# The last MLP's second matrix with activations stationary, and its residual with tokens on partitions

## The chip, the cores and the metric

The kernel runs on one core of one Trainium2 chip. The metric is the device time of one execution in microseconds (us). Three runs of the kernel before took 2691.77, 2692.02 and 2692.03 us; the median, 2692.02 us, is the time that the change is held against.

## The reference

A trunk of two layers over 256 tokens of width 2048, in float32. Each layer is a modulated RMS norm, a mixer (layer 0: gated DeltaNet heads beside band attention; layer 1: a Mamba-2 SSD mixer) with a gated residual, then another norm and a squared-ReLU MLP with a gated residual. The change touches only the second half of the last MLP:

```python
def sq_relu_mlp(h, w1, w2):                 # w1 2048 x 8192, w2 8192 x 2048
    a = jax.nn.relu(jnp.einsum('btd,df->btf', h, w1))
    return jnp.einsum('btf,fd->btd', a * a, w2)
...
        h = rms_norm(x, norm_mlp_w[layer]) * (1.0 + sc2) + sh2
        x = x + g2 * sq_relu_mlp(h, mlp_w1[layer], mlp_w2[layer])
```

The gate `g2` has one value for each of the 2048 features and is the same for all tokens.

## The kernel before

**Split operands.** Every large product runs in two parts for precision. A weight tile `raw` (128 x 2048 numbers, 1 MB, one DMA on the queue of SP) is split in two halves of 1024 columns: ACT casts `wh` (L342), DVE subtracts `wl = raw - wh` (L346). Activations are held in the same way as a high and a low part in a tile `u`. The product is high x high, high x low and low x high, so three products for each pair of tiles. All matmuls of such products are recorded at L332.

**One chunk of the last MLP.** A chunk is one `raw` tile: eight blocks of 128 rows by 256 columns. `c_item` (L592) works it off with the weights stationary: for each row block and each of two column blocks, one matmul `wh` against high and low activations side by side (512 columns move), and one `wl` against the high part (256 columns move). That is 16 matmuls of 512 columns and 16 of 256, and 32 weight loads. `c_blocks` pairs two chunks (rows r = 0 and r = 1) for one output block of 256 features, `pw`, which has features on partitions and tokens along the row. In chunk r = 0 the order is `wh`, then `wl`; in chunk r = 1 it is `wl`, then `wh`, so the trace shows runs of 32 matmuls of each kind.

**The MLP's loop** (`mlp`, L1516). The 8192 hidden features go by in four parts f. In each part, 16 chunks of `w1` make eight tiles `a` (each `relu2`: L1525 ACT, L1526 DVE, two ACT squares, a cast and a DVE subtraction), and 16 chunks of `w2` add to the output. The last MLP so has 64 chunks of `w1` and 64 of `w2`. The residual (`residual`, L951) is done for every output block in every f: four DVE instructions `x = pw * gate + x` at L958, where the gate is a column of numbers, one for each partition. In the last f the blocks go out by DMA (L960).

**Order of the work.** A chunk's load and split are emitted one chunk ahead of its matmuls. `raw` tiles, and the tiles `mraw` of the modulation (`mod_job`, a 1 MB load at L463 and one DVE product at L466 each), share one pool of four buffers; a load is issued when DVE has let go of the buffer four loads back. `wh` has four buffers, `wl` five. The modulation that ends in the gate of this MLP, `mod[2, ("mlp", 1)]`, is spread over f = 0: 16 loads, `pump` issues one about every four ticks, and `need` forces it when a residual wants columns that are not ready. Small jobs that PE, DVE and ACT do between chunks are Python generators, stepped from a list `bg` while the matmuls are emitted; a scheduler then sets the place of each instruction on its engine. SP issues DMAs strictly in its own order. The program gives SP's DMAs eight completion counters in turn, and a DMA first waits until the last one that had its counter has landed.

**The end.** The last chunk does all matmuls of its first column block, then the residual of that block, then the second column block. Both column blocks lie in one tile `pw`, two banks of PSUM.

Of the kernel before, what the change touches and what calls it, by code (L numbers as in the profile page):

```python
# [10 lines left out]
F32 = mybir.dt.float32  # L11
# [101 lines left out]
class Trunk:  # L113
# [88 lines left out]
    def back(self, gen):  # L202
        t = Task(gen)
        self.bg.append(t)
        return t
# [345 lines left out]
        self.emit(Item(load.finish, run, after, self.still > 0))  # L551
        self.still -= 1

    def a_item(self, ps, src, act, first, last, after=None, whole=False):

        load, ws = self.loader(src, whole)

        def run():
            o_, (u, x) = ps(), act()
            for hf, (wh, wl) in enumerate(self.tiles(ws, 512)):  # L560
                for n in range(4):
                    k, t = (n % 2, n // 2) if last and hf else (n // 2, n % 2)
# [385 lines left out]
        return get  # L948


    def residual(self, ps, cb, key, last, final=False, fs=(0, 1)):  # L951

        nc = self.nc
        self.need(2, key, 2 * cb + 2)
        g, x, b = self.mod[2, key], self.x[cb // 2], cb % 2
        for f in fs:
            for n in range(2):
                self.last = nc.vector.scalar_tensor_tensor(x[:, 2 * b + f], ps[:, f, n], g[:, 2 * cb + f : 2 * cb + f + 1], x[:, 2 * b + f], op0=ALU.mult, op1=ALU.add)  # L958
            if final:
                nc.sync.dma_start(self.out[cb // 2, :, b * 512 + f * 256 : b * 512 + f * 256 + 256], x[:, 2 * b + f])  # L960
        if last and not final:
# [554 lines left out]
    def mlp(self, layer, acts, after=None):  # L1516

        nc = self.nc
        w1, w2 = self.i["w1"][layer], self.i["w2"][layer]
        NF = DFF // 2048  # L1520

        def relu2(ps, early):
            p = self.unit(F32R, [P, 2, 2, SEQ])
            lo = self.s2([P, 2, SEQ], tag="rs")
            nc.scalar.copy(lo, ps[:, :, 1])  # L1525
            nc.vector.tensor_tensor(lo, ps[:, :, 0], lo, op=ALU.add)  # L1526
# [33 lines left out]
    def mlp_rate(self, layer):  # L1560
        self.rate = 0.377 if layer == 0 else 0.25
# [226 lines left out]
def pack(inputs):  # L1788
# [4 lines left out]
    def chunks(w, width=512):  # L1793
# [50 lines left out]
```

## Time and profile before

| what | value |
|---|---|
| median of three runs | 2692.02 us |
| the profiled execution | 2691.54 us |
| its span (first to last instruction of the program) | 2689.8 us |
| PE busy | 2635.2 us, 98% of the span |
| DVE busy | 2151.9 us, 80% |
| ACT busy | 1348.2 us, 50% |
| granted TensorE clock | 0.999 |

The profile is one execution. A span of busy time is not a rate: matmuls overlap, so each record of a 512-column matmul lasts about 390 ns while one starts every 227 ns. Where the text needs a rate, it takes the distance between starts. "Idle before" is the time in which an engine did nothing ahead of an instruction, with the instruction that let it go on. SPq is the queue of SP, which only issues DMAs; a DMA's landing is told in the list of DMAs.

### The profile page before, as it was taken

The numbers are of one execution on the slowest core, as the hardware profiler recorded it, in microseconds if no ns is written. First come the engines' busy times: TensorE is split into PE (matmuls) and PEld (weight loads), VectorE is DVE, ScalarE is ACT, GpSimd is POOL, SyncE is SP. The second block draws the span as 40 slices with busy tenths as digits, with TensorE's granted clock in tenths as the row PEclk, the third lists the DMA queues.
The fourth block names the chain that finished last, engine by engine and source line by source line (L and its number), as shares of the span: only waits on it lengthen the run. The fifth ranks groups of instructions, "written<-read, shape, count | busy, mean of one in ns | idle before, by whom it ended". The sixth has DMA issues, their size and how long they took to land.

```text
span 2689.8 us, 40012 instructions
## 1 busy us (share of the span) xinstructions
PE 2635.2 (98%) x15834; PEld 2324.1 (86%) x15834; DVE 2151.9 (80%) x3106; ACT 1348.2 (50%) x1990; POOL 24.3 (1%) x98
## 2 busy tenths in 40 slices
PE   5999999999999999999999999999999999999999
PEld 4887989988888888888888888888888888888888
DVE  7998998997888888889889876888797855555554
ACT  3445455456345354454556544655455354453452
POOL 1000000000000000000000000000000000000000
PEclk9999999999999999999999999999999999999999
DMA  9986487868899898988566655655567855555553
GB/s 344 352 327 234 170 307 275 322 235 293 313 345 328 328 332 330 333 331 312 179 207 220 219 204 185 207 175 188 208 236 293 325 188 188 188 188 188 191 193 134
DMA packets 100459, 680.08 MB, mean 253 GB/s; under 512 B 11184, under 2 KB 14512, under 8 KB 19376
## 3 DMA queue, kind: packets, MB, share of 16 engines
q1 hardware_dynamic: 95376, 669.07, 68.6%
q10 hardware_dynamic: 4896, 8.46, 1.0%
q8 instruction: 124, 2.03, 0.3%
q14 instruction: 63, 0.52, 0.1%
HBM read 675.33 MB, written 2.16 MB: 252 GB/s over the span
## 4 chain that ended last, share of the span: by engine, by line
PE 90%; DVE 7%; ACT 2%; issue 1%; DMA 1%; DVEq 0%; SPq 0%; ACTq 0%
PE pw L332 71%; PE pg L332 12%; PE pm L335 3%; PE pm L332 2%; DVE wl L346 2%; DVE mraw L466 2%; PE pm L339 1%; DVE u L1619 0%; ACT wh L342 0%; DVE hf L893 0%; DVE u L1017 0%; DMA raw<-in_w_ab_dram 0%; ACT pm L1075 0%; DVE u L896 0%; ACT pm L1218 0%
## 5 line engine op out<-in xcount | busy, mean ns | idle before, releaser
L346 DVE TENSOR_TENSOR wl<-raw,wh 128x1024 fp32r<-128x1024 f32 x870 | 1053.8, 1223 | 433.4 <-ACT wh L342 430.9
L342 ACT CAST wh<-raw 128x1024 fp32r<-128x1024 f32 x870 | 905.0, 1050 | 980.8 <-PE pw L332 676.6
L332 PE MATMUL pw<-u,wh 128*128 128x512 f32 x5584 | 1318.8, 391 | 2.6 <-DVE u L896 1.3
L332 PEld LDWEIGHTS pw<-u,wh 128*128 128x128 f32 x5584 | 1032.5, 188 | 209.3 <-issue 1.9
L332 PEld LDWEIGHTS pw<-u,wl 128*128 128x128 f32 x5584 | 702.1, 191 | 21.0 <-DVE wl L346 1.1
L332 PE MATMUL pw<-u,wl 128*128 128x256 f32 x5584 | 711.0, 283 | 0.7 <-DVE wl L346 0.7
L466 DVE SCALAR_TENSOR_TENSOR mraw<-mraw,crow 128x2048 f32<-128x2048 f32 x192 | 438.8, 2287 | 8.6 <-DMA mraw<-in_mod_dram 8.4
L332 PE MATMUL pg<-wh,u 128*128 128x512 f32 x864 | 282.1, 398 | 0.0
L332 PEld LDWEIGHTS pg<-wh,u 128*128 128x128 f32 x864 | 162.0, 188 | 33.2 <-issue 1.0
L958 DVE SCALAR_TENSOR_TENSOR x<-pw,mod,x 128x256 f32<-128x256 f32 x352 | 161.9, 480 | 32.4 <-PE pw L332 30.0
L332 PE MATMUL pg<-wl,u 128*128 128x512 f32 x432 | 169.7, 393 | 0.4 <-DVE wl L346 0.2
L332 PE MATMUL pg<-u,wh 128*128 128x256 f32 x672 | 124.5, 286 | 0.0
L332 PEld LDWEIGHTS pg<-u,wh 128*128 128x128 f32 x672 | 105.5, 192 | 0.3
L332 PEld LDWEIGHTS pg<-wl,u 128*128 128x128 f32 x432 | 81.3, 188 | 18.2 <-DVE wl L346 1.9
L332 PE MATMUL pg<-u,wl 128*128 128x256 f32 x336 | 95.6, 284 | 0.1
L332 PE MATMUL pm<-u,wh 128*128 128x256 f32 (+1 forms) x340 | 64.1, 292 | 19.2 <-ACT wh L342 19.2
L332 PEld LDWEIGHTS pm<-u,wh 128*128 128x128 f32 x340 | 54.3, 199 | 20.3 <-ACT wh L342 20.0
L332 PEld LDWEIGHTS pg<-u,wl 128*128 128x128 f32 x336 | 64.4, 192 | 0.3 <-DVE wl L346 0.3
L1017 DVE SCALAR_TENSOR_TENSOR u<-pad,cst,u 128x256 f32<-128x256 f32 x144 | 61.6, 481 | 1.0 <-ACT u L1011 0.7
L1525 ACT COPY rs<-pw 128x512 f32<-128x512 f32 x64 | 36.8, 576 | 34.5 <-PE pw L332 34.5
L895 ACT ACTIVATE u<-hf,mod 128x256 fp32r<-128x256 f32 x64 | 29.3, 501 | 47.2 <-DVE hf L893 47.2
L1526 DVE TENSOR_TENSOR rs<-pw,rs 128x512 f32<-128x512 f32 x64 | 43.9, 686 | 9.9 <-ACT rs L1525 9.9
(298 smaller groups left out, 1520.5 us busy)
## 6 DMA issues: line engine op xcount, KB each, us to landing
raw<-in_w_dram SPq DMA_DIRECT2D x256, 1024.0 KB, 5.4
mraw<-in_mod_dram SPq DMA_DIRECT2D x192, 1024.0 KB, 6.3
raw<-in_w_ab_dram SPq DMA_DIRECT2D x56, 1024.0 KB, 6.3
raw<-in_w_ssd_dram SPq DMA_DIRECT2D x48, 1024.0 KB, 4.8
raw<-in_w_sz_dram SPq DMA_DIRECT2D x32, 1024.0 KB, 4.9
raw<-in_wo_ssd_dram SPq DMA_DIRECT2D x32, 1024.0 KB, 4.9
raw<-in_wo_ab_dram SPq DMA_DIRECT2D x16, 1024.0 KB, 6.0
sE<-sd_rowd ACTq DMA_DIRECT2D x32, 256.0 KB, 3.9
```

Source lines behind the costliest of these rows:

```text
L332: return self.nc.tensor.matmul(o, a, b, start=start, stop=stop, skip_group_check=True)
L335: self.nc.tensor.matmul(o, lhsT, rhs, start=True, stop=True, skip_group_check=True)
L339: return self.nc.tensor.transpose(o, a, self.anti if flip else self.ident[:k, :k])
L342: a = self.nc.scalar.copy(hi, src)
L346: b = self.nc.vector.tensor_tensor(lo, src, hi.bitcast(F32), op=ALU.subtract)
L466: x = nc.vector.scalar_tensor_tensor(raw, raw, 1.0, self.crow, op0=ALU.mult, op1=ALU.mult, accum_out=t[:, f : f + 1])
L895: nc.scalar.activation(hi, h[:, f], AF.Identity, bias=shift[:, col])
L958: self.last = nc.vector.scalar_tensor_tensor(x[:, 2 * b + f], ps[:, f, n], g[:, 2 * cb + f : 2 * cb + f + 1], x[:, 2 * b + f], op0=ALU.mul ...
L1017: nc.vector.scalar_tensor_tensor(h, pad[:, f, 1 + q : 257 + q], w[:, q, j : j + 1], h, op0=ALU.mult, op1=ALU.add)
L1525: nc.scalar.copy(lo, ps[:, :, 1])
L1526: nc.vector.tensor_tensor(lo, ps[:, :, 0], lo, op=ALU.add)
```

## The change

Layer 1's `w2` is packed anew, as 64 chunks of four row blocks by 512 columns (`w2t`), and is worked off by `a_item`, an existing routine, through a new `w2_tokens`. There the activations are stationary and the weights move: for each of four row blocks and each of two blocks of 128 tokens, three matmuls of 512 columns (high x `wh`, high x `wl`, low x `wh`). That is 24 matmuls of 512 columns and 24 loads in place of 32. An output tile `pg` now has tokens on partitions and 512 features along the row; it takes four chunks (k = 0 to 3) of one feature group n, and there are four groups.

So x must have tokens on partitions too. `to_tokens` does that in the background, from the fourth block of `w1` in f = 0: 16 DVE transposes of 32 x 32 squares (128 x 256 each), 32 DMAs that write the result to DRAM, 32 DMAs that read it back into x in pieces of 128 bytes. `gate_rows` turns the gate into rows: per group n one small transpose on PE, an ACT copy, a DMA to DRAM and a DMA that spreads the row over 128 partitions. The residual `residual_tok` is then two DVE instructions per token block instead of one: product with the gate row, and sum. In the last chunk, the two token blocks have a PSUM tile each; the first one's residual is done while the second is multiplied. The output leaves in eight DMAs of 256 KB instead of 16 of 128 KB.

```diff
+            if mid:
+                halves = self.tiles(ws, 512)
+                for t in range(2):
+                    ts = slice(t * P, t * P + P)
+                    for hf, (wh, wl) in enumerate(halves):
+                        for k in range(2):
+                            self.mmx(o_[t], u[hf][:, k, 0, ts], wh[:, k], False, False)
+                            self.mmx(o_[t], u[hf][:, k, 0, ts], wl[:, k], False, False)
+                            self.mmx(o_[t], u[hf][:, k, 1, ts], wh[:, k], False, hf == k == 1)
+                        yield
+                    if t == 0:
+                        mid()
+                return
...
+    def to_tokens(self):
+        nc = self.nc
+        def back(n, scr):
+            cells = scr.rearrange("i f a t -> i (f a) t")
+            to = self.x[n].rearrange("p f t -> p (f t)").rearrange("p (t m j) -> p t m j", t=2, j=32)
+            for t in range(2):
+                for q in range(4):
+                    c = t * P + 32 * q
+                    nc.sync.dma_start(to[32 * q : 32 * q + 32, t], cells[:, :, c : c + 32])
+                yield
+        old = None
+        for n in range(4):
+            scr = self.dram_p.tile([32, 4, 4, SEQ], F32, tag=f"xt{n}", name=f"x_tok{n}")
+            ys = []
+            for h in range(2):
+                ys.append(self.s2([P, 2, SEQ], tag="xy"))
+                for f in range(2):
+                    nc.vector.transpose(ys[h][:, f], self.x[n][:, 2 * h + f])
+                yield
+            if old:
+                yield from back(*old)
+            for h in range(2):
+                for a in range(4):
+                    nc.sync.dma_start(scr[:, 2 * h : 2 * h + 2, a], ys[h][32 * a : 32 * a + 32])
+            yield
+            old = n, scr
+        yield
+        yield
+        yield from back(*old)
+    def gate_rows(self, key):
...
+            ps = self.pm()[:4, 0]
+            self.tr(ps, self.mod[2, key][:, 4 * n : 4 * n + 4])
+            g = self.s2([P, P], tag="gr")
+            nc.scalar.copy(g[:4], ps)
+            row = self.dram_p.tile([4, P], F32, tag=f"grow{n}", name=f"gate_row{n}")
+            nc.sync.dma_start(row, g[:4])
+            yield
+            yield
+            self.grow.append(self.s2([P, 512], tag="gw"))
+            nc.sync.dma_start(self.grow[n], row.rearrange("f p -> (f p)").unsqueeze(0).to_broadcast([P, 512]))
+    def residual_tok(self, ps, n, key, final, ts=(0, 1)):
...
+            v = self.s2([P, 512], tag="rt")
+            nc.vector.tensor_tensor(v, ps[t], self.grow[n], op=ALU.mult)
+            nc.vector.tensor_tensor(x[:, t], v, x[:, t], op=ALU.add)
+            if final:
+                nc.sync.dma_start(self.out[n, :, 512 * t : 512 * t + 512], x[:, t])
...
+                if cb == 3 and layer == 1 and f == 0:
+                    self.grow = []
+                    self.turned = [self.back(self.to_tokens()), self.back(self.gate_rows(key))]
...
+            if layer == 1:
+                self.w2_tokens(w2, f, NF, lambda n, a=a: a[n].finish(), key)
+                continue
```

The first place to look at is SP's order in f = 0, while `w1` is still under way. Before, loads of weights (`raw`) and of the modulation (`mraw`) stand alone there:

```order
L509 DMA raw_18919<-in_w_dram 128x2048
L509 DMA raw_18972<-in_w_dram 128x2048
L463 DMA mraw_18998<-in_mod_dram 128x2048
L509 DMA raw_19016<-in_w_dram 128x2048
L509 DMA raw_19069<-in_w_dram 128x2048
```

Now, at the same place, with `xy` the transposed squares, `x_tok` the DRAM copy, and `x_79`, `x_80` the first two of x's four tiles:

```order
L509 DMA raw_18919<-in_w_dram 128x2048
L509 DMA raw_18994<-in_w_dram 128x2048
L463 DMA mraw_19024<-in_mod_dram 128x2048
L990 DMA x_tok_18938<-xy_18939 32x2x256 x4
L990 DMA x_tok_18938<-xy_18942 32x2x256 x4
L990 DMA x_tok_18974<-xy_18975 32x2x256 x3
L974 DMA x_79<-x_tok_18938 32x16x32 x8
L990 DMA x_tok_18974<-xy_18975 32x2x256
L990 DMA x_tok_18974<-xy_18991 32x2x256 x4
L509 DMA raw_19054<-in_w_dram 128x2048
L974 DMA x_80<-x_tok_18974 32x16x32 x4
L509 DMA raw_19118<-in_w_dram 128x2048
```

The load `raw_19054` (it was `raw_19016`) now has 24 small DMAs ahead of it, and the next, `raw_19118` (it was `raw_19069`), four more. A little further on, with what each DMA waits for (DMAHW0 to DMAHW7 are the eight counters), stands:

```order
L974 DMA x_80<-x_tok_18974 32x16x32 [waits DMAHW1_49]
L974 DMA x_80<-x_tok_18974 32x16x32 [waits DMAHW2_49]
L463 DMA mraw_19148<-in_mod_dram 128x2048 [waits DMAHW3_49,DVE_49]
L990 DMA x_tok_19073<-xy_19074 32x2x256 [waits DMAHW4_49,DVE_49]
L990 DMA x_tok_19073<-xy_19074 32x2x256 [waits DMAHW5_49]
L990 DMA x_tok_19073<-xy_19074 32x2x256 [waits DMAHW6_49]
L990 DMA x_tok_19073<-xy_19074 32x2x256 [waits DMAHW7_49]
L990 DMA x_tok_19073<-xy_19098 32x2x256 [waits DMAHW0_49,DVE_49]
L990 DMA x_tok_19073<-xy_19098 32x2x256 [waits DMAHW1_49]
L990 DMA x_tok_19073<-xy_19098 32x2x256 [waits DMAHW2_49]
L990 DMA x_tok_19073<-xy_19098 32x2x256 [waits DMAHW3_49]
L509 DMA raw_19178<-in_w_dram 128x2048 [waits DMAHW4_49]
```

The last write before the load `raw_19178` has the counter of the 1 MB load `mraw_19148`, eight DMAs ahead of it.

The second place is DVE's order in the same stretch. Before, with L346 the splits of weights, L466 the modulation's products and L1526 the first step of a hidden tile:

```order
L346 TENSOR_TENSOR wl_18882<-raw_18875,wh_18881 128x1024
L466 SCALAR_TENSOR_TENSOR mraw_18901,mod_134<-mraw_18901,crow 128x2048
L346 TENSOR_TENSOR wl_18922<-raw_18919,wh_18921 128x1024
L346 TENSOR_TENSOR wl_18926<-raw_18919,wh_18925 128x1024
L1526 TENSOR_TENSOR rs_18947<-pw_18830,rs_18947 128x512
L466 SCALAR_TENSOR_TENSOR mraw_18998,mod_134<-mraw_18998,crow 128x2048
L346 TENSOR_TENSOR wl_18975<-raw_18972,wh_18974 128x1024
```

And now (L1526 has become L1602):

```order
L346 TENSOR_TENSOR wl_18882<-raw_18875,wh_18881 128x1024
L984 STREAM_TRANSPOSE xy_18939<-x_79 128x256 x2
L984 STREAM_TRANSPOSE xy_18942<-x_79 128x256 x2
L466 SCALAR_TENSOR_TENSOR mraw_18901,mod_134<-mraw_18901,crow 128x2048
L346 TENSOR_TENSOR wl_18922<-raw_18919,wh_18921 128x1024
L346 TENSOR_TENSOR wl_18926<-raw_18919,wh_18925 128x1024
L1602 TENSOR_TENSOR rs_18954<-pw_18830,rs_18954 128x512
L984 STREAM_TRANSPOSE xy_18975<-x_80 128x256 x2
L984 STREAM_TRANSPOSE xy_18991<-x_80 128x256 x2
L346 TENSOR_TENSOR wl_18997<-raw_18994,wh_18996 128x1024
```

The first tile's transposes stand right behind the split `wl_18882`, the second tile's behind one product, two splits and a step of a hidden tile; eight more follow within the next ten rows.

More of the change, by code (lines that the diff above doesn't have):

```diff
@@ L552, in b_item, with a_item @@
         self.still -= 1
-    def a_item(self, ps, src, act, first, last, after=None, whole=False):
+    def a_item(self, ps, src, act, first, last, after=None, whole=False, mid=None):
         load, ws = self.loader(src, whole)
@@ new lines, in gate_rows @@
+    def gate_rows(self, key):
+        nc = self.nc
+        for n in range(4):
+            while self.ready.get((2, key), 0) < 4 * n + 4:
+                yield False
+            yield
[6 more added lines that the diff above has]
+            yield
+            yield
+            self.grow.append(self.s2([P, 512], tag="gw"))
+            nc.sync.dma_start(self.grow[n], row.rearrange("f p -> (f p)").unsqueeze(0).to_broadcast([P, 512]))
@@ new lines, in residual_tok @@
+    def residual_tok(self, ps, n, key, final, ts=(0, 1)):
+        nc = self.nc
+        self.need(2, key, 4 * n + 4)
+        while len(self.grow) <= n:
+            self.turned[1].step()
+        x = self.x[n].rearrange("p f t -> p (f t)").rearrange("p (t c) -> p t c", t=2)
+        for t in ts:
+            v = self.s2([P, 512], tag="rt")
[3 more added lines that the diff above has]
+                nc.sync.dma_start(self.out[n, :, 512 * t : 512 * t + 512], x[:, t])
@@ L953, in residual @@
+    def residual(self, ps, cb, key, last, fs=(0, 1)):
         nc = self.nc
@@ L958, in residual @@
                 self.last = nc.vector.scalar_tensor_tensor(x[:, 2 * b + f], ps[:, f, n], g[:, 2 * cb + f : 2 * cb + f + 1], x[:, 2 * b + f], op0=ALU.mult, op1=ALU.add)
-            if final:
-                nc.sync.dma_start(self.out[cb // 2, :, b * 512 + f * 256 : b * 512 + f * 256 + 256], x[:, 2 * b + f])
-        if last and not final:
+        if last:
             self.sumsq(cb // 2, b, cb == 7, fs)
@@ L1518, in mlp @@
         nc = self.nc
-        w1, w2 = self.i["w1"][layer], self.i["w2"][layer]
+        w1, w2 = self.i["w1"][layer], self.i["w2t" if layer else "w2"]
         NF = DFF // 2048
@@ L1536, in mlp @@
         half = lambda n: acts(n // 2)[0][n % 2]
+        key = ("mlp", layer)
         for f in range(NF):
@@ L1552, in mlp @@
                 self.c_blocks(w2, (cb,), lambda n, a=a: a[n].finish(),
-                              lambda ps, cb, fs=(0, 1), f=f: self.residual(ps, cb, ("mlp", layer), f == NF - 1, layer == 1 and f == NF - 1, fs), f * 2,
+                              lambda ps, cb, fs=(0, 1), f=f: self.residual(ps, cb, key, f == NF - 1, fs), f * 2,
                               f == NF - 1 and cb == 7)
@@ L1558, in mlp, with w2_tokens, get @@
             self.early_item(after)
+    def w2_tokens(self, w, f, nf, act, key):
+        if self.turned[0] in self.bg:
+            self.bg.remove(self.turned[0])
+            self.turned[0].finish()
+        for n in range(4):
+            final = f == nf - 1
+            ps = []
+            def get(end=final and n == 3, ps=ps):
+                if not ps:
+                    self.room()
+                    ps.extend([self.pm([P, 512]) for _ in range(2)] if end else self.pg(True))
+                return ps
+            sink = lambda ts=(0, 1), ps=ps, n=n, final=final: self.residual_tok(ps, n, key, final, ts)
+            for k in range(4):
+                end = final and n == k == 3
+                self.still = max(self.still, int(final and n == 3))
+                self.a_item(get, w[4 * f + k, n], lambda k=k: ([act(2 * k), act(2 * k + 1)], None), k == 0, k == 3,
+                            None if k < 3 else (lambda s=sink: s((1,))) if end else sink, mid=(lambda s=sink: s((0,))) if end else None)
     def mlp_rate(self, layer):
@@ L1812, in pack @@
         "w_ssd": chunks(ssd[:, 4096:10240], 256), "w_dt": narrow(ssd[:, 10240:]), "wo_ssd": chunks(f("ssd_w_out")[0], 256),
-        "w1": np.stack([chunks(w, 256) for w in f("mlp_w1")]), "w2": np.stack([chunks(w, 256) for w in f("mlp_w2")]),
+        "w1": np.stack([chunks(w, 256) for w in f("mlp_w1")]), "w2": chunks(f("mlp_w2")[0], 256), "w2t": chunks(f("mlp_w2")[1]),
     }
@@ L1820, in unpack @@
 def unpack(y):
-    return np.ascontiguousarray(y.reshape(4, P, 4, SEQ).transpose(0, 2, 1, 3).reshape(D, SEQ).T).reshape(1, SEQ, D)
+    return np.ascontiguousarray(y.reshape(4, P, 2, 512).transpose(2, 1, 0, 3)).reshape(1, SEQ, D)
 @with_exitstack
```

1 line of the change is left out of this document (removed).

## Prediction

> **What bounds the kernel now.** I read the page's busy line and its chain of waits first.
>
> ```profile
> PE 2635.2 (98%) x15834; PEld 2324.1 (86%) x15834; DVE 2151.9 (80%) x3106; ACT 1348.2 (50%) x1990; POOL 24.3 (1%) x98
> PE 90%; DVE 7%; ACT 2%; issue 1%; DMA 1%; DVEq 0%; SPq 0%; ACTq 0%
> ```
>
> PE is busy for 98% of the span and carries 90% of the chain, so time is won by fewer or denser matmuls and lost by every wait of PE. Then I cut the last MLP into stages of about one part f each (columns: length, then PE, weight loads, DVE, ACT and POOL busy, clock, DMA share, GB/s).
>
> ```profile
> 1977.00:2062.00 85.00, 84.25 (x481) 74.14 (x482) 70.48 (x92) 53.72 (x76) 0.00 (x0) 1.00 0.73 266
> 2062.00:2150.00 88.00, 88.00 (x509) 77.98 (x509) 71.42 (x85) 35.53 (x36) 0.00 (x0) 1.00 0.83 310
> 2240.00:2328.00 88.00, 88.00 (x510) 78.00 (x509) 49.87 (x62) 35.71 (x36) 0.00 (x0) 1.00 0.55 192
> 2595.00:2690.00 95.00, 89.62 (x514) 78.80 (x512) 50.07 (x64) 32.71 (x33) 0.00 (x0) 1.00 0.41 144
> ```
>
> `w2` of f = 0, 1 and 3 is in the last three rows, `w1` of f = 0 in the first. PE never stops in the middle. DVE and DMA are far from full, except in f = 0 (the first two rows), where the modulation's loads run beside the weights: there DVE has 14.5 us spare in 85, and the DMA engines are busy 0.73 to 0.83 of the time. The change puts all its new DVE and DMA work into just these rows.
>
> **The matmuls: what 64 chunks gain.** PE's timeline in `w2` of f = 2 (start, length, then what) shows runs of 32, one kind after the other:
>
> ```profile
> 2565.55 4.00 PE L332 MATMUL pw<-u,wl 128*128 128x256 f32 x32
> 2569.38 7.44 PE L332 MATMUL pw<-u,wh 128*128 128x512 f32 x32
> 2576.66 4.00 PE L332 MATMUL pw<-u,wl 128*128 128x256 f32 x32
> 2580.49 7.44 PE L332 MATMUL pw<-u,wh 128*128 128x512 f32 x32
> ```
>
> Starts are what counts: 2576.66 - 2569.38 = 7.28 us for 32 matmuls of 512 columns, 227.5 ns each; 2580.49 - 2576.66 = 3.83 us for 32 of 256, 119.7 ns each. Half the columns cost more than half: a fixed part of 2 x 119.7 - 227.5 = 12 ns sits on each matmul. Two chunks take 11.11 us, one takes 5.555. The new form exists already in layer 1's mixer, where `a_item` runs three chunks without a break:
>
> ```profile
> 1779.59:1795.91 16.32, 16.32 (x72) 13.33 (x71) 0.00 (x0) 0.00 (x0) 1.00 0.66 221
> ```
>
> 16.32 us for 72 matmuls is 226.7 ns each, and 24 of them make 5.440 us. Both forms move 12,288 columns a chunk; the new one has eight matmuls fewer. Gain: 64 x (5.555 - 5.440) = 7.4 us, all on the path.
>
> **The end.** The timeline of the last microseconds:
>
> ```profile
> 2679.55 2.00 PE L332 MATMUL pw<-u,wh 128*128 128x512 f32 x8
> 2682.63 4.50 SPq L960 DMA_DIRECT2D out_dram<-x  x2
> 2682.65 2.12 PE L332 MATMUL pw<-u,wh 128*128 128x512 f32 x8 [1.10 <-DVE x L958]
> 2684.61 1.11 PE L332 MATMUL pw<-u,wl 128*128 128x256 f32 x8
> 2685.76 1.00 DVE L958 SCALAR_TENSOR_TENSOR x<-pw,mod,x 128x256 f32<-128x256 f32 x2 [3.16 <-PE pw L332]
> ```
>
> The second column block waits for the residual of the first: eight matmuls need 8 x 0.2275 = 1.8 us from 2679.55, so 2682.65 is 1.3 us late. With a PSUM tile for each token block that wait goes; next late is nothing, the weights being split already. Then the tail: last residual 1.00 us now, two instructions of 512 columns then; and a last DMA of 256 KB, not 128.
>
> ```profile
> L1526 DVE TENSOR_TENSOR rs<-pw,rs 128x512 f32<-128x512 f32 x64 | 43.9, 686 | 9.9 <-ACT rs L1525 9.9
> out_dram<-x SPq DMA_DIRECT2D x16, 128.0 KB, 2.1
> ```
>
> 2 x 0.686 - 1.00 = +0.4 us, and I put the doubled DMA at +0.3 (between 0 and a second 2.1). End in all: -1.3 + 0.7 = -0.6 us.
>
> **DVE's balance, off the path.** Each part f loses 32 residual instructions and gains 16 of 128x512.
>
> ```profile
> L958 DVE SCALAR_TENSOR_TENSOR x<-pw,mod,x 128x256 f32<-128x256 f32 x128 | 58.7, 479 | 9.2 <-PE pw L332 8.2
> L846 DVE TENSOR_TENSOR ss<-ss,sq 128x256 f32<-128x256 f32 x48 | 20.6, 429 | 0.9
> L466 DVE SCALAR_TENSOR_TENSOR mraw<-mraw,crow 128x2048 f32<-128x2048 f32 x192 | 438.8, 2287 | 8.6 <-DMA mraw<-in_mod_dram 8.4
> L342 ACT CAST wh<-raw 128x1024 fp32r<-128x1024 f32 x870 | 905.0, 1050 | 980.8 <-PE pw L332 676.6
> L346 DVE TENSOR_TENSOR wl<-raw,wh 128x1024 fp32r<-128x1024 f32 x870 | 1053.8, 1223 | 433.4 <-ACT wh L342 430.9
> ```
>
> 128 x 0.479 = 61 us go, 64 x 0.686 = 44 come; that buys nothing, since DVE waits there anyway. A residual of 2.7 us in one piece stands between the two splits of a chunk that PE wants 5.4 us later, so it costs nothing either; without that lead it would cost its 2.7 us once in four chunks. No row shows a transpose. At the shape 128x256 other instructions take 0.43 to 0.48 us; I take 0.45 (0.3 to 0.9 as bounds), so 16 cost 7.2 us of the 14.5 spare.
>
> **SP's queue in f = 0: what it costs.** Here PE can be made to wait. SP's timeline before:
>
> ```profile
> 2011.59 0.33 SPq L509 DMA_DIRECT2D raw<-in_w_dram  x1
> 2014.50 0.33 SPq L463 DMA_DIRECT2D mraw<-in_mod_dram  x1
> 2016.67 3.56 SPq L509 DMA_DIRECT2D raw<-in_w_dram  x2
> ```
>
> and PE's at the place where those weights are used:
>
> ```profile
> 2024.83 7.44 PE L332 MATMUL pw<-u,wh 128*128 128x512 f32 x32
> 2032.11 4.00 PE L332 MATMUL pw<-u,wl 128*128 128x256 f32 x32
> 2043.22 4.00 PE L332 MATMUL pw<-u,wl 128*128 128x256 f32 x32
> ```
>
> The load issued at 2016.67 (`raw_19016`, now `raw_19054`) is a chunk of the kind that starts with `wl`: the second half of the run at 2032.11, so from 2034.0. From landing to the first `wl` go a cast and a split, 1.05 + 1.22 us; it must land by 2031.7. Small DMAs, back to back, leave SP at this pace, and large ones land so (list of DMAs from 2005 to 2062, and the page's row of the `ssd` weights: KB each, median us to landing):
>
> ```profile
> 0.80 1.80 SPq L1575 DMA_DIRECT2D x<-in_x_dram  x4
> 2.65 0.67 SPq L463 DMA_DIRECT2D mraw<-in_mod_dram  x1
> DMA packets 2360, 17.25 MB, mean 303 GB/s; under 512 B 256, under 2 KB 256, under 8 KB 256
> q1 hardware_dynamic: 2357, 17.21, 81.1%
> raw<-in_w_dram SPq DMA_DIRECT2D x11, 1024.0 KB, 5.9
> raw<-in_w_ssd_dram SPq DMA_DIRECT2D x48, 1024.0 KB, 4.8
> mraw<-in_mod_dram SPq DMA_DIRECT2D x5, 1024.0 KB, 6.4
> ```
>
> One issue takes 1.80 / 4 = 0.45 us. Now the walk. `mraw` leaves at 2014.50, the first tile's four transposes end near 2016.3, and eight writes have left SP by 2018.6. The next three writes need the second tile's first two transposes; on DVE those stand behind 2.29 (L466) + 2 x 1.22 (splits) + 0.69 (hidden tile), so 2016.3 + 5.4 + 0.9 = 2022.6, and SP stands still for 4 us. From there 16 small DMAs: 16 x 0.45 = 7.2, so the load leaves at 2029.8 instead of 2016.67 and lands between 4.8 and 5.9 us later, at 2035.1 in the middle. 2035.1 - 2031.7: PE waits 3.4 us. With transposes of 0.3 us, issues of 0.33 (the shortest above) and a landing of 4.8 it would be 2022.3 + 5.3 + 4.8 - 2031.7 = 0.7; with read-backs at 0.67 (the longest issue on SP, the first `mraw`), transposes of 0.9 us and a landing of 5.9 it would be 2023.5 + 9.0 + 5.9 - 2031.7 = 6.7.
>
> The next chunk of that kind, `raw_19178`, is wanted from 2045.1, plus what PE is late by then. In front of it stand four read-backs that wait for the writes' landing (about 2.1 us), `raw_19118`, four more, `mraw`, and eight writes; the last of these shares a counter with `mraw`. So 2029.8 + 0.5 + 2.1 + 9 x 0.45 = 2036.5 for `mraw`, 6.4 for its landing, one issue: the load leaves at 2043.4, lands at 2048.9, first `wl` at 2051.2, against 2045.1 + 3.4. Another 2.7 us at these values, 0 if the small DMAs are a little quicker. After that the demand is later (chunks that start with `wh`, and the first `w2t` chunk at 2061.8), and I reckon nothing more. Both waits: 3.4 + 2.7 = 6 us; since each is a last-to-land argument at median landings, I take 5.5, with 1 and 14 as ends.
>
> What hides x's read-back itself: it is wanted only at the end of group 0's fourth chunk, over 80 us after the first transposes.
>
> **The gate rows.** Four transposes on PE, and one ACT copy each.
>
> ```profile
> L339 PE MATMUL pm<-ident,u 128*128 128x128 f32 x176 | 25.3, 273 | 0.0
> ```
>
> 25.3 / 176 = 0.14 us each: 0.5 us in all. They also make PE wait for DVE's sum of the modulation. For groups 0 to 2 that sum is done a chunk earlier; the last stands on PE four matmuls into `w1` of f = 1, while its `mraw` can leave only when the split of the last chunk of `w2` has freed a buffer: landing 4.8 to 6.4, product 2.29, against 5.44 + 0.9 us of matmuls from that chunk's start. I take 1.0 us of waiting (0 to 3). Queued behind it is all of PE; the row itself is wanted a chunk pair later.
>
> **The sum** against the profiled execution of 2691.54 us: -7.4 (matmuls) - 0.6 (end) + 5.5 (SP's queue) + 0.5 + 1.0 (gate) = -1.0, so 2690.5. The median of the runs is 0.5 above that execution: **2691.0 us**. No change means within 0.2%, 5.4 us, about what a measurement of this kernel can tell.
>
> **The rivals.**
>
> *The queue keeps ahead* (chance 0.28). ACT's timeline has that load's cast:
>
> ```profile
> 2026.87 1.05 ACT L342 CAST wh<-raw 128x1024 fp32r<-128x1024 f32 x1 [3.60 <-PE pw L332]
> ```
>
> The load issued at 2016.67 lands, at the median of 5.9, 4.3 us before its cast starts, at 2026.87, and buffers may absorb more than my walk grants; SP's 13 us of delay then costs 1 us and the gate nothing: -7.4 - 0.6 + 1.0 + 0.5 = -6.5, 2685.5 us. For it: in the stages' middle rows PE is busy for 88.00 us of 88.00. Against it: the walk finds 24 DMAs ahead of one load.
>
> *The squares choke the DMA rings: slower* (0.21). 2 MB go out in pieces of 1 KB and come back as 16,384 pieces of 128 bytes, in a stretch where queue 1 is busy 81% already and moves 17.25 MB in 57 us. At the rate of that row (46 us of ring time for 17.25 MB) 4 MB cost 11 us, just the 57 - 46 = 11 spare.
>
> ```profile
> q10 hardware_dynamic: 4896, 8.46, 1.0%
> ```
>
> At this queue's mean packet (1.0% of 16 x 2689.8 us over 4896, 88 ns) the pieces alone cost 16,384 x 88 / 16 = 90 us. It decides from about 12 us of PE waiting on; with 14 for the queue and 2 for the gate the time is 2692.0 - 7.5 + 16 = 2700.5 us. The Trainium skill, "DMA: Bandwidth & Descriptors", section "Specifications", says that pieces under 512 bytes fall below line rate, as each write becomes a read and a write; no row here shows pieces of 128 bytes.
>
> *Columns alone count* (0.05). If a matmul's cost were its columns, the form would not matter, the 7.4 us would not come, and the time would be 2691.0 + 7.4 = 2698.4 us. Against it stand 227.5 and 119.7 ns above. The Trainium skill, "TensorE: Matmul & The Clock Gate", section "Back-to-back issue gap", puts only 2.5 ns on top of the columns' time. By it a chunk would save 20 ns and the 64 chunks 1.3 us, for an estimate of 2697.1 us; the rows show 12 ns, and I go by them.
>
> **How the numbers follow.** The forecast has the rest, 0.46; it spans 2686.5 to 2697. Faster by over 0.2%: the first rival, 0.28. Slower: the second and third, less a little that falls inside, 0.25. Within: 0.47. The range goes from 2684.0 (no wait at all) to 2701.0, and leaves out some 0.05 below and 0.1 above.
>
> **What would show it.** In the profile after: runs of `pg` matmuls at 226 to 228 ns, a chunk at 5.44; no idle time of PE at the last block; PE idle before `wl` near 2034 and 2045, ended by DVE, with the matching load late on SP behind L974 and L990; a pause of PE at the fourth gate transpose. I am wrong if PE's waits in f = 0 sum to under 2 us or over 12, if transposes take over 0.9 us, or if a chunk of `w2t` does not come to 5.44.

## The result, and the profile after

The changed kernel takes 2704.4 us (median of six runs, 2702.5 to 2708.5), the one before 2691.9 us (six runs, 2689.9 to 2694.2). The ratio is 1.0049, with a 95% interval from 1.0039 to 1.0060: 12.5 us slower by the medians. The profiled execution has a span of 2703.5 us against 2689.8. The matmuls gave what was forecast; PE's waits in f = 0 cost about three times what was forecast, and there are more of them than were forecast.

The page's busy line and chain now:

```profile
PE 2635.2 (97%) x15326; PEld 2301.9 (85%) x15326; DVE 2147.8 (79%) x3058; ACT 1349.1 (50%) x1994; POOL 24.4 (1%) x98
PE 89%; DVE 6%; ACT 2%; DMA 1%; issue 1%; SPq 0%; DVEq 0%; ACTq 0%
```

PE has 508 instructions fewer (512 fewer matmuls, four new transposes) and the same busy time: records of overlapping matmuls don't show the gain. The distance between starts shows it. Two windows over `w2t` of f = 1 and `w1` of f = 2, each from the stage's first start to the next stage's first start:

```profile
2259.74:2346.78 87.04, 87.04 (x385) 72.07 (x384) 48.40 (x47) 35.93 (x36) 0.00 (x0) 1.00 0.55 188
2346.78:2435.69 88.91, 88.91 (x514) 78.75 (x512) 49.10 (x50) 48.82 (x60) 0.00 (x0) 1.00 0.55 195
```

Sixteen chunks take 87.04 us in the new form, 5.440 each; sixteen of the old form take 88.91, 5.557 each.

What was given back stands between 2033 and 2082. PE's timeline there:

```profile
2031.44 2.07 PE L332 MATMUL pw<-u,wl 128*128 128x256 f32 x16
2039.82 3.78 PE L332 MATMUL pw<-u,wl 128*128 128x256 f32 x16 [6.31 <-DVE wl L346]
2043.40 4.46 PE L332 MATMUL pw<-u,wh 128*128 128x512 f32 x16
2049.48 3.92 PE L332 MATMUL pw<-u,wh 128*128 128x512 f32 x16 [1.62 <-ACT wh L342]
...
2055.41 0.27 PE L339 MATMUL pm<-ident,mod 128*4 128x128 f32 x1
2058.23 3.68 PE L332 MATMUL pw<-u,wl 128*128 128x256 f32 x16 [2.55 <-DVE wl L346]
...
2067.18 3.92 PE L332 MATMUL pw<-u,wh 128*128 128x512 f32 x16 [1.62 <-ACT wh L342]
...
2080.55 0.49 PE L332 MATMUL pg<-wh,u 128*128 128x512 f32 x1 [1.62 <-ACT wh L342]
2081.81 0.50 PE L332 MATMUL pg<-wl,u 128*128 128x512 f32 x1 [0.77 <-DVE wl L346]
```

PE waits six times, 14.5 us by the bracketed idle time. By starts it is 15.8 us: a record ends some 0.16 us after the start that would follow it, and the gate's transpose waits 0.26. And the matmuls behind a long wait are slow: the 16 of 256 columns from 2039.82 take 3.58 us to the next start, 224 ns each where they took 120. The same stretch by windows (the column behind POOL is the granted clock):

```profile
2033.50:2039.80 6.30, 0.01 (x1) 0.00 (x0) 1.26 (x2) 1.99 (x2) 0.00 (x0) 0.85 0.99 271
2039.80:2045.00 5.20, 5.18 (x21) 4.84 (x22) 1.10 (x1) 0.00 (x0) 0.00 (x0) 0.53 1.03 276
2049.50:2053.20 3.70, 3.70 (x16) 3.09 (x17) 3.26 (x4) 2.66 (x4) 0.00 (x0) 1.00 1.03 306
2058.20:2062.00 3.80, 3.77 (x18) 3.72 (x19) 1.11 (x1) 0.00 (x0) 0.00 (x0) 0.55 1.02 310
2082.00:2085.80 3.80, 3.80 (x11) 2.94 (x11) 3.37 (x3) 1.69 (x3) 0.00 (x0) 0.55 1.00 425
```

Behind the waits of 6.31 and 2.55 us the granted clock is 0.53 and 0.55; behind the one of 1.62 at 2049.48 it is 1.00. Behind the last two waits together, 1.62 and 0.77, it is 0.55 again. Counted by starts, such stretches cost 6.1 us in all.

SP's timeline shows where the weights were. L509 loads weights, L990 and L974 are the new small writes and read-backs:

```profile
2013.83 0.33 SPq L463 DMA_DIRECT2D mraw<-in_mod_dram  x1
2014.48 7.65 SPq L990 DMA_DIRECT2D x_tok<-xy  x11
2022.30 6.12 SPq L974 DMA_DIRECT2D x<-x_tok  x8
2028.47 2.52 SPq L990 DMA_DIRECT2D x_tok<-xy  x5
2031.03 0.43 SPq L509 DMA_DIRECT2D raw<-in_w_dram  x1
2032.29 2.55 SPq L974 DMA_DIRECT2D x<-x_tok  x4
2034.89 1.98 SPq L509 DMA_DIRECT2D raw<-in_w_dram  x1
```

The load that left at 2016.67 leaves at 2031.03, behind the 24 small DMAs. In the row of plain loads that the prediction used, an issue took 0.45 us; the eight read-backs take 6.12 / 8 = 0.77 on average. The list of DMAs from 2005 to 2062 says whether the weights also travel more slowly:

```profile
raw<-in_w_dram SPq DMA_DIRECT2D x7, 1024.0 KB, 6.3
```

6.3 us in place of 5.9: the load leaves 14 us late and travels 0.4 us longer. (In e9 below, with the same 64 DMAs, the median is 5.6, so the 0.4 is not shown to be theirs.)

ACT's timeline shows something else. Its queue has the copy of a finished hidden block (L1601), or of a gate row (L1007), ahead of the next weights' cast:

```profile
2047.89 0.59 ACT L1601 COPY rs<-pw 128x512 f32<-128x512 f32 x1 [8.44 <-PE pw L332]
2048.38 2.00 ACT L342 CAST wh<-raw 128x1024 fp32r<-128x1024 f32 x2
...
2055.72 0.26 ACT L1007 COPY gr<-pm 4x128 f32<-4x128 f32 x1 [3.50 <-PE pm L339]
2055.88 1.99 ACT L342 CAST wh<-raw 128x1024 fp32r<-128x1024 f32 x2
```

The copy waits for PE's block (or the gate's transpose) to end, the cast stands behind the copy, and PE waits for the cast. Five of the six waits end in this way, all but the first. Before, the casts stood ahead of the copies; for the block of the copy at 2047.89 the order was:

```profile
2039.80 1.06 ACT L342 CAST wh<-raw 128x1024 fp32r<-128x1024 f32 x1 [0.76 <-PE pw L332]
2040.76 0.57 ACT L1525 COPY rs<-pw 128x512 f32<-128x512 f32 x1
```

So two theories stood against each other: the loads come late (SP's queue), or they are there in time and ACT's changed order holds up their casts.

The end is as planned. PE does not stop, and the second block's product starts 0.2 us after the last matmul's start plus its distance.

```profile
2698.45 0.39 PE L332 MATMUL pm<-wh,u 128*128 128x512 f32 x1
2698.87 0.69 DVE L1024 TENSOR_TENSOR rt<-pm,gw 128x512 f32<-128x512 f32 x1 [1.30 <-PE pm L332]
```

From the last matmul's start plus its distance to the end of the span it is 2703.5 - 2698.7 = 4.8 us; before it was 2689.8 - 2685.6 = 4.2, with a stop of 1.3 ahead.

The sum over the two profiles: -7.4 (matmuls) + 0.6 - 1.3 (end) + 15.8 (waits) + 6.1 (half clock) + 0.5 (gate transposes) - 0.7 (the last MLP starts at 1976.7 in place of 1977.4) = 13.6, against 2703.5 - 2689.8 = 13.7.

### The profile page after: what moved, and what is told of

Read it like the earlier page. It is cut to its first block, busy times and chain, and to the rows that moved or that the text cites. A ratio compares the mean times of both kernels' runs of the same rounds, so it can differ in the third digit from the quotient of the medians.

```text
span 2703.5 us, 38959 instructions
## 1 busy us (share of the span) xinstructions
PE 2635.2 (97%) x15326; PEld 2301.9 (85%) x15326; DVE 2147.8 (79%) x3058; ACT 1349.1 (50%) x1994; POOL 24.4 (1%) x98
## 4 chain that ended last, share of the span: by engine, by line
PE 89%; DVE 6%; ACT 2%; DMA 1%; issue 1%; SPq 0%; DVEq 0%; ACTq 0%
PE pw L332 57%; PE pg L332 24%; PE pm L335 4%; PE pm L332 3%; DVE mraw L466 2%; DVE wl L346 2%; PE pm L339 1%; ACT wh L342 1%; DMA raw<-in_w_ab_dram 1%; DVE u L1724 0%; DVE hf L906 0%; DVE u L909 0%; ACT pm L1151 0%; DMA raw<-in_w_dram 0%; ACT pm L1294 0%
## 5 line engine op out<-in xcount | busy, mean ns | idle before, releaser
L346 DVE TENSOR_TENSOR wl<-raw,wh 128x1024 fp32r<-128x1024 f32 x870 | 1052.1, 1221 | 425.0 <-ACT wh L342 422.5
L332 PE MATMUL pw<-u,wh 128*128 128x512 f32 x4560 | 1081.2, 391 | 4.7 <-ACT wh L342 3.2
L332 PEld LDWEIGHTS pw<-u,wh 128*128 128x128 f32 x4560 | 842.5, 188 | 173.8 <-ACT wh L342 4.1
L332 PEld LDWEIGHTS pw<-u,wl 128*128 128x128 f32 x4560 | 577.8, 192 | 28.0 <-DVE wl L346 10.5
L332 PE MATMUL pw<-u,wl 128*128 128x256 f32 x4560 | 587.0, 284 | 9.6 <-DVE wl L346 9.6
L332 PE MATMUL pg<-wh,u 128*128 128x512 f32 x1824 | 579.9, 394 | 1.6 <-ACT wh L342 1.6
L466 DVE SCALAR_TENSOR_TENSOR mraw<-mraw,crow 128x2048 f32<-128x2048 f32 x192 | 438.1, 2284 | 7.6 <-DMA mraw<-in_mod_dram 7.5
L332 PEld LDWEIGHTS pg<-wh,u 128*128 128x128 f32 x1824 | 342.9, 188 | 73.1 <-ACT wh L342 2.0
L332 PE MATMUL pg<-wl,u 128*128 128x512 f32 x912 | 357.1, 392 | 1.1 <-DVE wl L346 0.8
L332 PEld LDWEIGHTS pg<-wl,u 128*128 128x128 f32 x912 | 171.8, 188 | 38.3 <-DVE wl L346 3.1
L1036 DVE SCALAR_TENSOR_TENSOR x<-pw,mod,x 128x256 f32<-128x256 f32 x224 | 102.8, 478 | 21.8 <-PE pw L332 20.4
L1601 ACT COPY rs<-pw 128x512 f32<-128x512 f32 x64 | 37.0, 578 | 62.9 <-PE pw L332 62.9
L1602 DVE TENSOR_TENSOR rs<-pw,rs 128x512 f32<-128x512 f32 x64 | 43.9, 685 | 30.2 <-ACT rs L1601 30.2
```

What stands on the lines that cost most here:

```text
L332: return self.nc.tensor.matmul(o, a, b, start=start, stop=stop, skip_group_check=True)
L346: b = self.nc.vector.tensor_tensor(lo, src, hi.bitcast(F32), op=ALU.subtract)
L466: x = nc.vector.scalar_tensor_tensor(raw, raw, 1.0, self.crow, op0=ALU.mult, op1=ALU.mult, accum_out=t[:, f : f + 1])
```

## The experiments

Every kernel ran beside the kernel before on the same chip, whose medians were 2691.3 to 2692.2 us; ratios are to it.

| run | what | us | ratio (95%) |
|---|---|---|---|
| | the changed kernel | 2704.4 | 1.0049 (1.0039 to 1.0060) |
| e1 | without the 64 DMAs | 2686.0 | 0.9973 (0.9963 to 0.9984) |
| e2 | the 64 DMAs on GpSimd's queue | 2717.2 | 1.0087 (1.0073 to 1.0100) |
| e3 | ACT's order put back, gate copy too | 2710.1 | 1.0063 (1.0050 to 1.0075) |
| e4 | x turned on PE, no DMAs | 2687.8 | 0.9984 (0.9976 to 0.9993) |
| e5 | the 64 DMAs made tiny | 2698.4 | 1.0026 (1.0016 to 1.0036) |
| e6 | without the 32 read-backs | 2692.1 | 1.0004 (0.9995 to 1.0012) |
| e7 | everything one part f later | 2704.9 | 1.0049 (1.0035 to 1.0062) |
| e8 | the kernel before with six pauses of PE | 2724.1 (one run) | |
| e9 | ACT's order put back, gate rows later | 2702.1 | 1.0039 (1.0027 to 1.0052) |
| e10 | e9 without the read-backs | 2687.7 | 0.9985 (0.9976 to 0.9994) |

**e1, the DMAs left out.**

```diff
-                    nc.sync.dma_start(to[32 * q : 32 * q + 32, t], cells[:, :, c : c + 32])
+                    pass
...
-                    nc.sync.dma_start(scr[:, 2 * h : 2 * h + 2, a], ys[h][32 * a : 32 * a + 32])
+                    pass
```

> Leaves out the 64 DMAs that write the transposed squares to DRAM and read them back, so x keeps its old order and the output is not the reference's; the transposes on DVE, the gate rows and the new matmuls stay. It prices everything else of the change. Queue theory (the DMAs make the loss, through SP's queue and the order that ACT got because of it): no waits of PE from 2030 to 2090, time 2684 us (2682 to 2687), that is the 7.4 us of the matmuls and 0.6 of the end. Rival (the gate rows or DVE's transposes make PE wait): still above 2690 us, with PE waits of some 3 us where the gate's transposes stand.

2686.0 us, 6.3 below the kernel before (4.3 to 10 by the interval), where 8 was expected. Between 2030 and 2090 PE does not wait. So the 64 DMAs, with the order that they bring, are the whole loss, 2704.43 - 2685.96 = 18.5 us, and the rest of the change gains what was reckoned, within the interval.

**e2, the same DMAs on another queue.** `nc.sync.dma_start` in `to_tokens` becomes `nc.gpsimd.dma_start`, twice.

> The same 64 DMAs, the same bytes in the same pieces of 128 bytes, but issued on GpSimd's queue; nothing is left out. Queue theory: SP's loads keep their places and ACT its old order, so 2684 to 2686 us. Ring theory (2 MB in pieces of 128 bytes fill the DMA engines and delay the weights whoever issues them): PE still waits some 15 us in f = 0, 2698 to 2705 us.

Neither theory's number: 2717.2 us. But the place of the loss has moved. While w1 and the first `w2t` chunks run, with SP's queue clear, PE works nearly all the time:

```profile
2005.00:2090.00 85.00, 83.94 (x447) 1.00 0.84 306
```

What follows is new. GpSimd's timeline shows one read-back at a time, some 5 us apart, and DVE's shows a residual that waits for x:

```profile
2025.27 0.67 POOL L974 DMA_DIRECT2D x<-x_tok  x1 [2.92 <-DMA x_tok<-xy]
2031.37 0.65 POOL L974 DMA_DIRECT2D x<-x_tok  x1 [5.43 <-issue]
```
```profile
2197.87 0.69 DVE L1025 TENSOR_TENSOR x<-rt,x 128x512 f32<-128x512 f32 x1 [9.59 <-DMA x<-x_tok]
```

The last of the 32 leaves at 2195.41. The splits queue on DVE behind the waiting residual, and PE behind the splits. So this run does not weigh the pieces of 128 bytes: only 11 of the 32 read-backs had left by 2090. It shows that SP's loads are in time when nothing small stands ahead of them, and that x's read-back, harmless on SP, is late on a queue that issues one in 5 us.

**e3, ACT's order put back.**

```diff
-            nc.scalar.copy(lo, ps[:, :, 1])
+            c = nc.scalar.copy(lo, ps[:, :, 1])
+            if behind:
+                self.put_behind(c, self.last_cast)
...
-            nc.scalar.copy(g[:4], ps)
+            self.put_behind(nc.scalar.copy(g[:4], ps), self.last_cast)
```

> The changed kernel with SP's queue as it is; only ACT's order in f = 0 is put back: the copies of blocks 5 to 7 and of the gate row stand behind the casts of the weights that are loaded by then. Order theory (from 2047 on PE waits because a cast stands on ACT behind a copy that itself waits for PE, or for the gate's transpose): the waits near 2047, 2055, 2065 and 2078 go, 9 us with some 4 us of half clock behind them, the one at 2033 (6.3 us and its half clock) stays: 2692 us (2689 to 2695). Load theory (weights come late, the order on ACT only follows): no gain, 2702 to 2705 us.

2710.1 us, slower than the changed kernel: the order theory falls in this form. The edit had a flaw of its own, which SP's timeline shows:

```profile
2054.36 0.54 SPq L974 DMA_DIRECT2D x<-x_tok  x1
2062.34 0.33 SPq L1009 DMA_DIRECT2D gate_row<-gr  x1
```

The write of the gate row stood at SP's head for 7.4 us, until ACT had made the copy that I had put behind a cast; the next weights stood behind it. e9 mends this.

**e4, x turned on PE.** `to_tokens` becomes:

```diff
+            for t in range(2):
+                ps.append(self.pm([P, 512]))
+                for m in range(4):
+                    self.tr(ps[t][:, P * m : P * m + P], self.x[n][:, m, P * t : P * t + P])
+            for t in range(2):
+                nc.vector.tensor_copy(x[:, t], ps[t])
+            yield
```

> x is turned by 32 transposes of 128x128 on PE and eight DVE copies out of PSUM, in place of DVE's squares and the 64 DMAs; nothing is left out. Queue theory: no waits from loads, PE pays 32 x 0.11 to 0.14 us = 3.5 to 4.5, so 2684 + 4 = 2688 us (2686 to 2691). Rival (gate rows or the new form itself cost): above 2692 us.

2687.8 us, as expected: 4.5 us faster than the kernel before (2692.2 in that comparison; 1.9 to 6.5 by the interval) and 16.6 faster than the changed one. PE pays for 32 transposes, which start 0.11 us apart in a run, and never waits from 2030 on for weights. Beside e1, which has no re-layout at all, the kernel is 1.8 us slower.

```profile
L339 PE MATMUL pm<-ident,x x32: 270/272/273, 1978.0 to 2025.7; 128*128 128x128 f32 x32
L975 DVE COPY x<-pm x8: 675/681/692, 2000.2 to 2026.4; 128x512 f32<-128x512 f32 x8
```

(The first row's numbers are the lasting of one record, least, median and most.) With nothing left out, this version beats both kernels.

**e5, the same DMAs with little in them.**

```diff
-                    nc.sync.dma_start(to[32 * q : 32 * q + 32, t], cells[:, :, c : c + 32])
+                    nc.sync.dma_start(to[32 * q : 32 * q + 32, t, 0], cells[:, 0, c : c + 32])
...
-                    nc.sync.dma_start(scr[:, 2 * h : 2 * h + 2, a], ys[h][32 * a : 32 * a + 32])
+                    nc.sync.dma_start(scr[:, 2 * h, a], ys[h][32 * a : 32 * a + 32, 0])
```

> The same 64 DMAs at the same places of SP's queue, but each write moves half of its bytes and each read-back one piece of 128 bytes per partition in place of 16, so 1/16 of the pieces; the output is not the reference's. Place theory (each weight load leaves late since up to 24 issues and their waits stand ahead of it): the loads leave as late as in the changed kernel, PE's first wait stays near 5 to 6 us, time 2698 to 2704 us. Bytes theory (the 16,384 pieces hold the DMA engines): most of the loss goes, 2686 to 2691 us.

2698.4 us, the place theory's lower end: with a sixteenth of the pieces of 128 bytes (and writes of half the size), 12.5 of the 18.5 us are still lost. SP's timeline:

```profile
2018.60 3.67 SPq L974 DMA_DIRECT2D x<-x_tok  x8
2022.36 4.33 SPq L990 DMA_DIRECT2D x_tok<-xy  x8
2026.74 0.42 SPq L509 DMA_DIRECT2D raw<-in_w_dram  x1
```

An issue of a small read-back takes 3.67 / 8 = 0.46 us, not 0.77. The first late load leaves at 2026.74, not 2031.03; that is still 10 us later than before, but PE waits only 1.55 us for it in place of 6.31, where 5 to 6 had been expected. So the pieces' part is at most 6.0 us, since the writes shrank too. What the pieces cost shows first in the issues, 0.31 us each. A wait for the eight counters does not explain these: from 2022 to 2028.5 the changed kernel's read-backs land 2.5 us after their issue, long before eight more have been issued.

**e6, the read-backs left out.** The first of e1's two edits alone.

> The 32 writes stay, the 32 read-backs in pieces of 128 bytes are left out, so x keeps its old order and the output is not the reference's. Place theory: 16 writes stand ahead of the first late load in place of 24 DMAs, and no others between the loads but eight at a time: the loss of 18 us halves, 2692 to 2697 us. Bytes theory (pieces of 128 bytes): 2686 to 2689 us.

2692.1 us, the low end of the place theory's range: the 32 writes cost 6.2 us, the 32 read-backs 12.3. In this trace the order theory has its case after all. The weights had landed by 2062.2 (issue 2056.46, landing 5.8 later), and their cast starts at 2065.35:

```profile
2064.86 0.59 ACT L1601 COPY rs<-pw 128x512 f32<-128x512 f32 x1 [6.26 <-PE pw L332]
2065.35 1.99 ACT L342 CAST wh<-raw 128x1024 fp32r<-128x1024 f32 x2
```

**e7, one part f later.** Part f = 0 of the second matrix keeps the old form; the squares start with the first block of `w1` in f = 1.

```diff
-                if cb == 3 and layer == 1 and f == 0:
+                if cb % 8 == 0 and layer == 1 and f == 1:
...
-            if layer == 1:
-                self.w2_tokens(w2, f, NF, lambda n, a=a: a[n].finish(), key)
+            if layer == 1 and f:
+                self.w2_tokens(w2t, f, NF, lambda n, a=a: a[n].finish(), key)
```

> The first part f = 0 of the second matrix stays in the old form; the squares, the 64 DMAs on SP and the gate rows come in f = 1, where no loads of the modulation run beside the weights; the new form takes 48 chunks. Nothing is left out. Theory that the loss needs the modulation's loads beside it (queue and DMA engines both full): 48 x 0.115 + 0.6 = 6.1 us won, little lost: 2686 to 2689 us. Theory that the 64 DMAs on SP delay loads wherever they stand: PE waits again for some 10 us, 2695 to 2703 us.

2704.9 us, 2 us above the range of the second theory, so the modulation's loads are not needed for the loss. PE waits again, now in f = 1; the two longest waits for weights:

```profile
2221.22 3.78 PE L332 MATMUL pw<-u,wl 128*128 128x256 f32 x16 [3.15 <-DVE wl L346]
...
2247.03 2.52 PE L332 MATMUL pw<-u,wh 128*128 128x512 f32 x6 [4.32 <-ACT wh L342]
```

With 48 chunks in the new form and no loss the kernel would stand at 2691.3 - 48 x 0.115 - 0.7 = 2685.1 us, so the same 64 DMAs (and the gate rows) cost some 20 us here.

**e8, pauses.**

```diff
+        for _ in range(getattr(self, "rep", 0)):
+            self.nc.scalar.copy(hi, src)
+        self.rep = 0
         a = self.nc.scalar.copy(hi, src)
```

> The kernel before, in which six casts of weights in the last MLP are repeated 6 to 12 times, so that PE waits at six places for a growing time (some 2 to 9 us). Clock theory (a wait above some 2 us is followed by 3 to 5 us in which matmuls start 213 and 427 ns apart in place of 120 and 227, so it costs some 2 us more than its own length): such stretches stand behind the longer waits, none behind those under 1.7 us. Rival (the half clock in the changed kernel has another cause, the DMAs): matmuls go on at 120 and 227 ns behind every wait.

PE's timeline at four of the six places (of each, the run of 16 matmuls behind the pause), then windows behind the first, second and last of them:

```profile
2131.22 3.96 PE L332 MATMUL pw<-u,wh 128*128 128x512 f32 x16 [2.17 <-ACT wh L345]
2313.63 5.52 PE L332 MATMUL pw<-u,wh 128*128 128x512 f32 x16 [2.94 <-ACT wh L345]
2452.90 6.23 PE L332 MATMUL pw<-u,wh 128*128 128x512 f32 x16 [4.02 <-ACT wh L345]
2647.83 6.07 PE L332 MATMUL pw<-u,wh 128*128 128x512 f32 x16 [7.25 <-ACT wh L345]
```
```profile
2131.20:2135.20 4.00, 3.98 (x18) 3.29 (x19) 4.00 (x5) 1.05 (x1) 0.00 (x0) 1.00 0.65 250
2313.50:2317.60 4.10, 3.97 (x11) 3.16 (x12) 3.99 (x4) 0.96 (x2) 0.00 (x0) 0.62 0.15 26
2647.70:2652.00 4.30, 4.17 (x10) 3.30 (x11) 4.19 (x4) 0.43 (x2) 0.00 (x0) 0.50 0.16 32
```

The clock theory holds behind the longer pauses, with no re-layout in the kernel: 16 matmuls take 3.96 us behind 2.17 us of waiting, and 5.52 to 6.23 behind 2.94 to 7.25. In this run a wait from 2.94 us on costs 1.6 to 2.3 us more than its length, whatever its length.

The other traces show that between 1.5 and 2.9 us the length alone does not settle it. Matmuls started 213 or 427 ns apart, in place of 120 and 227, for 2 to 3 us behind 2.55 us (the changed kernel and e5), behind 2.40 (e3), behind 1.62 and 0.77 in close succession (the changed kernel and e6), and behind 1.55 in e5. The clock stayed at 1.00 behind 2.89 us in e7 (2201.10 to 2204.90), behind 2.55 in e6 (2047.70 to 2051.50) and behind 2.17 here. What decides between them is not shown. e5's row behind 1.55 us:

```profile
2035.80:2039.00 3.20, 3.20 (x12) 2.72 (x11) 2.36 (x2) 1.41 (x2) 0.00 (x0) 0.50 0.66 250
```

The Trainium skill, "TensorE: Matmul & The Clock Gate", section "What's actually happening", says that TensorE's clock goes to half after an idle window of about 3.4 us and back after as long of steady work, and that the window runs freely. By that figure no wait under 3.4 us would have been expected to trip it; here 2.94 did, and so did some waits from 1.55 us on, so the traces set the limit lower and leave it open.

**e9 and e10, the order again, without e3's flaw.** ACT's copies as in e3; the gate rows start after the last block of `w1`, so that neither their copy nor their DMA stands in this stretch. e10 also leaves out the read-backs.

```diff
-                    self.turned = [self.back(self.to_tokens()), self.back(self.gate_rows(key))]
+                    self.turned = [self.back(self.to_tokens())]
+                if cb == 7 and layer == 1 and f == 0:
+                    self.turned.append(self.back(self.gate_rows(key)))
```

> The changed kernel, nothing left out, all 64 DMAs on SP; ACT's copies of blocks 5 to 7 stand behind the casts of the weights in hand, and the gate rows start only after the last block of w1, so that no copy of a gate row stands ahead of a cast there and no gate DMA holds up SP. Order theory (of the 18 us that the DMAs cost, what lies behind 2045 us comes from casts that stand on ACT behind a copy): the wait near 2033 stays (6 us and 2 of half clock), the others go, 2692 to 2696 us. Late-load theory (behind 2045 the loads themselves come late): PE waits for loads at the same places, 2701 to 2708 us.

> As before it, and the 32 read-backs left out as well (x keeps its old order, the output is not the reference's). The run without read-backs took 2692.1 us, and in its trace PE waits 2.7 us for the gate's copy and 1.8 and 1.0 for casts behind a copy, with weights that had landed 3 to 4 us earlier, then half clock. Order theory: these waits go, 2684 to 2687 us, as without any of the DMAs. Late-load theory: no gain, 2690 to 2693 us.

With all DMAs in place the order is worth 2.4 us (2702.1 against 2704.4, intervals overlapping), and the time lies in the late-load theory's range. PE's waits are now 6.43, 1.89, 1.00 and 3.86 us. ACT now waits for the weights themselves, at the places where it waited for a copy:

```profile
2052.37 1.99 ACT L342 CAST wh<-raw 128x1024 fp32r<-128x1024 f32 x2 [8.66 <-DMA raw<-in_w_dram]
2069.10 1.99 ACT L342 CAST wh<-raw 128x1024 fp32r<-128x1024 f32 x2 [6.48 <-DMA raw<-in_w_dram]
```

Without the read-backs the same edit is worth 4.5 us (2687.7 against 2692.1), just above the order theory's range. Both are true, one behind the other: as long as the read-backs stand on SP the loads are the last to come, and ACT's order costs little; once they are gone, the order is what is late next.

So the 18.5 us divide like this: 1.7 for the writes with a good order (e10 over e1, which leaves the gate rows where they were), 4.5 for ACT's order that the DMAs brought with them (e6 over e10), 6.3 for the read-backs' places in the queue (e5 over e6; e5's writes are half as large, so this is a lower bound) and 6.0 for their pieces (the changed kernel over e5, for the same reason an upper bound). Each step is uncertain by some 3 us, as the intervals of its two runs are. Counted against the kernel before of each run's own comparison, the steps are 2.5, 4.5, 6.3 and 5.5.

## Why the prediction was wrong, point by point

- **Matmuls, -7.4 us: right.** 5.440 us a chunk, as worked out; e1 has the gain without the loss. The rival that columns alone count is out.
- **The end, -0.6: right**, -0.7 by the profiles.
- **DVE's squares: right.** 0.40 us each, 0.45 taken, hidden.

```profile
L984 DVE STREAM_TRANSPOSE xy<-x x16: 395/401/435, 2013.7 to 2030.3; 128x256 f32<-128x256 f32 x16
```

- **The first wait: right in kind, half in size.** It was 6.3 us, not 3.4. The load left at 2031.03 where the walk said 2029.8; landing took 6.4 us, not 5.3 (the first cast is at 2037.46); and PE was 0.7 us earlier in this profile (2031.44 in place of 2032.11). The late departure comes from "One issue takes 1.80 / 4 = 0.45 us", a row of a plain load of x: a read-back whose 64 KB are 512 pieces takes 0.77. The squares hid part of that error: they were done sooner than the walk had them, so that the first read-back left at 2022.30 (2022.6 + 3 x 0.45 = 2023.9 by the walk).
- **"After that the demand is later ... and I reckon nothing more": the step that failed.** The walk stopped at the second load. The 64 DMAs hold SP for some 45 us between 2014 and 2077 (the first rows alone: 7.65 + 6.12 + 2.52 + 2.55 us), while PE asks for a load every 5.5 us and each late load lets its buffer go late. A queue that has fallen behind stays behind until the small DMAs are through. PE waited at 2049, 2058, 2067 and 2080 besides: 5.5 us were put down for the queue's waits, 15.8 measured for all. e9 shows that the late loads alone do it: with ACT's copies out of the way the waits still come to 13.2 us, the longest after the first being 3.86 at 2071. By the prediction's own sign, waits over 12 us, it was wrong.
- **The second wait forecast, 2.7 us: near in size by luck.** The wait of 2.55 at 2058 stands near its place, but ends at a cast that stood behind the copy of the gate row. The same 2.55 us stands behind that copy in e5 and e6, whose loads left at other times; in e9, without the copy there, the load alone makes 1.89.
- **Half clock: not in the sum at all.** 6.1 us. The granted clock was 1.00 in every row that I had quoted, so I priced a wait at its length. e8 shows such a price without the DMAs.
- **The gate, 1.5 us: wrong place.** The fourth transpose, which I feared, did not wait; the first did (0.26 us), and its copy on ACT stood ahead of a cast, with the 2.55 us just named behind it.
- **ACT's order was not looked at.** I compared SP's and DVE's orders of instructions, not ACT's, where the casts had gone behind the copies. Putting it back won only 2.4 us (e9), since the loads were later still; without the read-backs it won 4.5.
- **The slower rival had the right sign and was nearest (2700.5 us), by another mechanism.** It put some 12 us and more of waiting down to the pieces; e5 leaves them 6 us at most, and most of the loss stays with the queue's order. That its number came near is luck. The result lies above the range, whose end of 2701.0 held 14 us of waits for SP and nothing for the clock. Left open: how the 6 us of the pieces divide between SP's longer issues and fuller DMA engines (busy 0.94 of the time from 2031 to 2055, 0.79 in e5).

## What to carry to other kernels

In this kernel a small DMA on the queue that also feeds the bottleneck cost its issue time, more with more pieces, for every load behind it. So walk the queue to the last small DMA and not only to the first late load, and look at the order on every engine that the delay can turn round. Price a stop of TensorE above its length: here every stop from 2.94 us on cost about 2 us more, and some shorter ones did too, so that several middling stops can be worse than their sum.

A layout change of 2 MB that takes PE an estimated 3.5 us (32 x 0.11) was cheaper by 16.6 us than one on engines with time to spare. The Trainium skill, "VectorE: DVE Perf Modes", section "Rules for kernel authors", sends a 128x128 transpose to TensorE where its target may be PSUM. e4 agrees.

## What the hardware did that I had not expected

- An issue on SP took 0.46 us on average for a read-back of 4 KB in 32 pieces and 0.77 us for one of 64 KB in 512 pieces (e5 and the changed kernel, the first eight of each; the issuing instruction's median is 0.42 and 0.63).
- GpSimd's queue issued the same read-back once in 5.5 us on average (32 from 2025 to 2195), SP once in 0.77.
- TensorE ran at half clock for 2 to 6 us behind every wait from 2.94 us on that these runs show in the last MLP. Behind waits of 1.55 to 2.9 us it sometimes did and sometimes did not: of two waits of exactly 2.55 us, in e5 and e6, one was followed by half clock and the other by full clock.
